# Chunk 0 of the Gram blocks at 64 columns, placed first in its group on the two borrowed PSUM banks

## The chip, the core and the metric

The kernel runs on one core of one Trainium2 chip. The metric is device time in microseconds (us), the median over several executions. Before the change it is 1001.87 us (three runs, 1001.54 to 1002.07).

## What is computed

One layer of a hybrid encoder block over 528 tokens (16 meta tokens and 512 real ones) of width 2048. One input projection feeds two branches: an RWKV-7 recurrence with 16 heads of 64, and a gated short convolution. Their outputs are concatenated and go through one output projection. The change touches only the recurrence, which per token and head is

```python
sa = einsum('bhvk,bhk->bhv', S, kk_t)
S  = S * w_t - sa[..., None] * b_t + v_t[..., None] * k_t
y_t = einsum('bhvk,bhk->bhv', S, r_t)
```

The first 16 tokens (the meta tokens) are dropped from the output, so for them only the state S matters, not y.

## The kernel before

**Chunks.** The recurrence is not run token by token. Tokens are laid out in `NCH` = 9 chunks of `CH` = 64: chunk 0 holds the 16 meta tokens and padding, chunks 1 to 8 the 512 real tokens. Heads are handled in 8 pairs; a pair fills the 128 partitions, one head on partitions 0 to 63 and the other on 64 to 127. `prepare(i)` makes for pair `i` two tiles: `ar` (decayed keys in half 0, receptance in half 1 of each chunk) and `bk` (two sets of decayed keys). For chunk 0 the receptance half is zeros: line 662 sets `ar[:, 0, 1]` to 0 with a memset on POOL.

**The Gram blocks.** For every chunk and head, `gram` multiplies 64 rows of `bk` (128 columns, the stationary weights) with 64 rows of `ar` (128 columns, streamed through) into a 128x128 block: 18 matmuls in float32 for each pair, which the trace records as 36 because each float32 matmul takes two passes. `masked` then multiplies the blocks with a causal mask on DVE and writes them to the SBUF tile `gt`. For chunk 0 the columns 64 to 127 of each block are zero before and after the mask, because the receptance half is zero, and nothing that is computed later reads those columns for its result.

**Where the blocks lie.** PSUM has eight banks. Pool `pm` has four of them (tag `main`) for the two accumulators of the running input projection and of the one before it; pool `pz` has two (`tz`); pool `pi` has one each of `misc` and `ser`. The nine chunks of one head take nine blocks of a quarter bank: four in a `tz` bank (`za`, chunks 0 to 3), four in `misc` or `ser` (`zc`, chunks 4 to 7) and the ninth in a bank borrowed from the projection (`ze`, chunk 8). With two heads that is six banks, two of them borrowed from `main`.

**What sets the order.** The order of TensorE's work is written by hand. The input projection (`main`, `steps`, line 328) is a generator that is stepped by `fill(ns)`, so that projection matmuls stand between the small steps of `prepare` and `invert`; a call fills a given number of modelled nanoseconds with them. A projection unit (names `ps_k`, `ps_r`, `ps_v`, `ps_g`, `ps_C` and so on) runs for about 11 us, then its one or two `main` banks are read by DVE (`scaled`, line 352), and the next unit needs free `main` banks. The queues of DVE, ACT and POOL are ordered by a planner at build time, from its own estimate of costs, priorities and of when each input is ready; `ahead()` and `tc.high_priority` raise priorities there. Each engine then runs its list in order.

**Lines that the change and the prediction speak of.** Line 677 is the `fill` ahead of the Gram group, line 703 the loop over chunks, lines 705 to 707 the masks, line 708 the `fill` behind them. Lines 714 to 718 are the next small products (`n2` into `misc` and `tz`, `zb` into `ser`), which need those banks back. Lines 746 and 751 send `gt` to DRAM by DMA: to the inversion of the 16x16 blocks, and to the store `opd`, from which the recurrence loads its operands. Lines 855 and 895, in `invert`, are the last reads of `gt` on TensorE; there are two `gt` buffers, one for even and one for odd pairs. Line 135 on POOL and DVE makes the low part of the projection's weights, out of what ACT casts in line 134. Line 460 sums squares at the start, with single-column float32 matmuls. Line 1005 is a product of the recurrence.

Of the kernel before, what the change touches and what calls it, by code (L numbers as in the profile page):

```python
# [9 lines left out]
F32 = mybir.dt.float32  # L10
# [8 lines left out]
P = 128  # L19
# [5 lines left out]
CH = 64  # L25
NCH = SEQ // CH + 1
# [51 lines left out]
def hymba_kernel(ctx: ExitStack, tc: tile.TileContext, xt, xtok, front, w_in, w_out, pv, lup, cst, msk, gf, out):  # L78
    nc = tc.nc
# [14 lines left out]
    def col(off, i=0):  # L94
        return pvt[:, off + i : off + i + 1]
# [69 lines left out]
    gmask = cs[:, C_GM : C_GM + 256].rearrange("p (h c) -> p h c", h=2)  # L165
    pm = ph1.enter_context(tc.tile_pool(name="pm", bufs=4, space=PSUM))
# [130 lines left out]
    with tc.issue_after(head):  # L297
        nc.vector.tensor_scalar(
            out=omm, in0=pvt[:, V_MU : V_MU + 33], scalar1=-1.0, scalar2=1.0, op0=ALU.mult, op1=ALU.add
        )  # L300
        for d, off in (
# [4 lines left out]
                out=d, in0=pvt[:, off : off + 8], scalar1=0.5, scalar2=None, op0=ALU.mult  # L306
            )
        nc.vector.tensor_scalar(
            out=hv[:, 4], in0=pvt[:, V_KA : V_KA + 8], scalar1=-0.5, scalar2=1.0, op0=ALU.mult, op1=ALU.add
# [241 lines left out]
    def fill(ns):  # L551
        while ns > 0:
            seen = len(ready)
            t = step()
            if t is None:
                return
            ns -= t
            if len(ready) > seen:
                ns += FW["evac"]
# [23 lines left out]
    def ahead():  # L583
        return tc.high_priority(offset=AHEAD)

    def c3(t):
        return t.rearrange("p (c s) -> p c s", s=CH)
# [39 lines left out]
    def prepare(i):  # L627
        p = i % 2
        until("k", i)
        k = got["k", i]  # L630
        ar = cq.tile([P, NCH, 2, CH], F32, tag="ar", name=f"ar{i}")
# [18 lines left out]
            out=bk[:, :, 1], in0=c3(k), scalar=hv[:, 2, i : i + 1], in1=c3(te), op0=ALU.mult, op1=ALU.mult  # L650
        )
        nc.gpsimd.tensor_scalar(
            out=ta, in0=ta, scalar1=hv[:, 3, i : i + 1], scalar2=hv[:, 4, i : i + 1], op0=ALU.mult, op1=ALU.add
        )
        nc.vector.scalar_tensor_tensor(
            out=ar[:, :, 0], in0=c3(k), scalar=col(V_KK, i), in1=e1[:, :, 0:CH], op0=ALU.mult, op1=ALU.mult
# [9 lines left out]
            out=ar[:, 1:NCH, 1], in0=c3(r), in1=e1[:, 1:NCH, 1 : CH + 1], op=ALU.mult  # L666
        )
        nc.vector.scalar_tensor_tensor(
            out=r, in0=r, scalar=hv[:, 5, i : i + 1], in1=ta[:, CH:LP], op0=ALU.mult, op1=ALU.mult
# [7 lines left out]
        fill(FW["gram_b" if p else "gram"] + shift)  # L677

        gt = cq.tile([P, 2, NCH, P], F32, tag=f"gt{p}", name=f"gt{i}")
        def gram(z, c, c0):  # L680
            for h, hs, ho in heads:
                nc.tensor.matmul(  # L682
                    z[h][:, c - c0],
                    bk[hs, c, h : h + 2, :].rearrange("p a s -> p (a s)"),
                    ar[hs, c].rearrange("p a s -> p (a s)"),
                    start=True, stop=True,
                )

        def masked(z, c0, c1):
            with ahead():  # L690
                for h in range(2):
                    nc.vector.tensor_tensor(  # L692
                        out=gt[:, h, c0:c1],
                        in0=z[h],
                        in1=gmask[:, h].unsqueeze(1).to_broadcast([P, c1 - c0, P]),
                        op=ALU.mult,
                    )


        za = [pz.tile([P, 4, P], F32, tag="tz", name=f"g{i}_0_{h}") for h in range(2)]  # L700
        zc = [pi.tile([P, 4, P], F32, tag=("misc", "ser")[h], name=f"g{i}_4_{h}") for h in range(2)]
        ze = [pm.tile([P, 1, P], F32, tag="main", name=f"g{i}_8_{h}") for h in range(2)]
        for c in range(NCH):
            gram((za, zc, ze)[c // 4], c, c // 4 * 4)
        masked(za, 0, 4)
        masked(zc, 4, 8)
        masked(ze, 8, 9)
        fill(FW["gram2"] - shift + 1300 * (i == 1) + 2000 * (i == 3))

        n2 = tr(f"n2{i}")  # L710
# [56 lines left out]
        def sub(x, r0, c0, dims):  # L767
            return bass.AP(tensor=x.tensor, offset=x.offset + r0 * 16 + c0, ap=[list(x.ap[0])] + dims)

        for m in (2, 4, 8):  # L770
            for b in range(16 // (2 * m)):
# [4 lines left out]
                    out=pq,  # L776
                    in0=sub(d, o, o + m, [[16, m], [0, m], [1, m]]),
                    in1=sub(y, o + m, o + m, [[0, m], [1, m], [16, m]]),
# [3 lines left out]
                    out=tq.rearrange("p (i j) -> p i j", i=m), in_=pq, op=ALU.add, axis=AX.X  # L782
                )
                nc.vector.tensor_tensor(
                    out=pq,
                    in0=sub(y, o, o, [[16, m], [0, m], [1, m]]),
                    in1=bass.AP(tensor=tq.tensor, offset=tq.offset, ap=[list(tq.ap[0]), [0, m], [1, m], [m, m]]),
# [274 lines left out]
    for i in range(0, NPAIR, 2):  # L1062
        invert([prepare(i), prepare(i + 1)])
# [155 lines left out]
    def here(t, n):  # L1219
        return xa[t][:, n * 512 : (n + 1) * 512] if n < 2 else xb[n - 2][:, t]  # L1220
# [151 lines left out]
    z = {}  # L1372
    for u, unit in enumerate(units):
        half, prod, g = unit
# [53 lines left out]
    with tc.manual_schedule(engines={mybir.EngineType.DVE, mybir.EngineType.Activation, mybir.EngineType.Pool}):  # L1428
# [16 lines left out]
        for part in range(2):  # L1445
# [7 lines left out]
            h = here(1, 2)[:, cols]  # L1453
# [73 lines left out]
```

## Time and profile before

| what | value |
|---|---|
| median of the runs | 1001.87 us |
| the profiled execution's own time | 999.8 us |
| its span, first to last instruction | 997.9 us |
| TensorE (PE) busy | 986.4 us, 99% of the span |
| DVE, ACT, POOL busy | 691.5, 412.7, 268.2 us |
| granted TensorE clock, mean | 0.997 of full speed |
| Gram matmuls (line 682) | 288 records in 8 groups, from 80.6 to 547.2 us |
| Gram masks on DVE (line 692) | 48: 32 of 128x512 and 16 of 128x128 |

A row of a timeline gives the start in us, the time in us until the last of the merged instructions ends, the engine (PE is the matmuls, PEld the weight loads), the line of the kernel, the operation with the tiles it writes and reads, shapes, and the count of merged records; a bracket is idle time before it and what ended it. Matmuls are pipelined: one record lasts longer than the distance to the next, so rates are read from the distance between starts.

### The profile page before, as it was taken

Reading aid. Unit: us, or ns where it says so; the run is one execution under the profiler, and the core shown is the slowest. Engines: PE = TensorE matmul, PEld = TensorE weight load, DVE = VectorE, ACT = ScalarE, POOL = GpSimd, SP = SyncE. Lnnn points to the kernel's source line nnn. Section 1 sums busy time; section 2 is a strip of 40 time slices with the busy share of each in tenths; the row PEclk is TensorE's granted clock in tenths of the full one; section 3 lists DMA queues with packets and bytes.
Section 4 is the critical chain, followed back from the end, with each engine's and each line's share of the span. In section 5 each row is a group of like instructions: output and inputs, shape, how many; then the busy total and the mean of one; then the engine's idle time right before and its main releaser. Section 6 shows DMA issues by size and latency. Waiting matters only on the chain.

```text
span 997.9 us, 22790 instructions
## 1 busy us (share of the span) xinstructions
PE 986.4 (99%) x9211; PEld 911.0 (91%) x9211; DVE 691.5 (69%) x1314; ACT 412.7 (41%) x770; POOL 268.2 (27%) x286
## 2 busy tenths in 40 slices
PE   9999999999999999999999999999999999999996
PEld 8999999999998999998999998989889898888885
DVE  7687975487765679735579735246555598999895
ACT  7554432353422534232534323233333325645553
POOL 0123323234322324222324222223242422011001
PEclk9999999999999999999999999999999999999998
DMA  9527485437683465854264854988783698698644
GB/s 337 155 70 198 112 218 150 115 105 179 149 226 108 107 178 128 221 148 118 84 180 119 224 142 125 355 259 281 219 262 94 195 260 229 212 297 218 143 102 168
DMA packets 184986, 179.48 MB, mean 180 GB/s; under 512 B 112177, under 2 KB 141617, under 8 KB 184369
## 3 DMA queue, kind: packets, MB, share of 16 engines
q1 hardware_dynamic: 182288, 169.12, 57.9%
q0 software_dynamic: 2304, 8.39, 4.9%
q8 instruction: 72, 1.18, 0.5%
q10 hardware_dynamic: 288, 0.52, 0.1%
q14 instruction: 34, 0.27, 0.1%
HBM read 139.28 MB, written 38.71 MB: 178 GB/s over the span
## 4 chain that ended last, share of the span: by engine, by line
PE 96%; DVE 1%; DMA 1%; issue 1%; POOL 0%; ACT 0%; DVEq 0%; POOLq 0%
PE ps_r L328 9%; PE ps_h L328 9%; PE ps_g L328 9%; PE ps_gc L328 9%; PE ps_B L328 9%; PE ps_v L328 9%; PE ps_C L328 8%; PE ps_k L328 8%; PE M L1243 8%; PE P L1243 4%; PE Q L1243 2%; PE g L682 2%; DMA ct<-opd 1%; PE ps_lora L328 1%; PE rz L958 1%; PE zs L1005 1%
## 5 line engine op out<-in xcount | busy, mean ns | idle before, releaser
L134 ACT CAST w<-wr 128x512 fp32r<-128x512 f32 x252 | 153.4, 619 | 281.0 <-PE ps_h L328 44.7
L135 POOL TENSOR_TENSOR w<-wr,w 128x512 fp32r<-128x512 f32 x119 | 165.8, 1395 | 371.5 <-ACT w L134 331.6
L135 DVE TENSOR_TENSOR w<-wr,w 128x512 fp32r<-128x512 f32 x133 | 99.2, 751 | 99.8 <-ACT w L134 99.6
L328 PE MATMUL ps_r<-xh,w 128*128 128x256 f32 (+1 forms) x512 | 95.2, 282 | 1.0 <-DVE gt L692 1.0
L328 PE MATMUL ps_k<-xh,w 128*128 128x256 f32 (+1 forms) x512 | 95.4, 284 | 0.0
L328 PE MATMUL ps_v<-xh,w 128*128 128x272 f32 (+1 forms) x512 | 95.4, 284 | 0.0
L328 PE MATMUL ps_h<-xh,w 128*128 128x258 f32 (+1 forms) x512 | 93.4, 282 | 0.0
L328 PE MATMUL ps_C<-xh,w 128*128 128x258 f32 (+1 forms) x512 | 93.2, 281 | 0.0
L328 PE MATMUL ps_g<-xh,w 128*128 128x258 f32 (+1 forms) x512 | 91.7, 280 | 0.0
L328 PE MATMUL ps_B<-xh,w 128*128 128x512 f32 x256 | 83.1, 394 | 0.0
L328 PEld LDWEIGHTS ps_r<-xh,w 128*128 128x128 f32 x512 | 80.2, 189 | 1.6 <-DVE gt L692 1.2
L328 PE MATMUL ps_gc<-xh,w 128*128 128x512 f32 x256 | 81.7, 393 | 0.0
L328 PEld LDWEIGHTS ps_k<-xh,w 128*128 128x128 f32 x512 | 80.3, 189 | 0.3
L328 PEld LDWEIGHTS ps_v<-xh,w 128*128 128x128 f32 x512 | 80.1, 189 | 0.3
L328 PEld LDWEIGHTS ps_C<-xh,w 128*128 128x128 f32 x512 | 79.6, 189 | 0.6
L328 PEld LDWEIGHTS ps_h<-xh,w 128*128 128x128 f32 x512 | 79.2, 189 | 0.7
L328 PEld LDWEIGHTS ps_g<-xh,w 128*128 128x128 f32 x512 | 79.2, 189 | 0.2
L328 PE MATMUL ps_k<-xl,w 128*128 128x256 f32 (+1 forms) x256 | 73.0, 285 | 0.0
L328 PE MATMUL ps_v<-xl,w 128*128 128x256 f32 (+1 forms) x256 | 72.5, 283 | 0.0
L328 PE MATMUL ps_g<-xl,w 128*128 128x256 f32 (+1 forms) x256 | 72.4, 283 | 0.0
L328 PE MATMUL ps_r<-xl,w 128*128 128x256 f32 (+1 forms) x256 | 72.1, 282 | 0.0
L328 PE MATMUL ps_C<-xl,w 128*128 128x256 f32 (+1 forms) x256 | 71.9, 281 | 0.0
(312 smaller groups left out, 2205.8 us busy)
## 6 DMA issues: line engine op xcount, KB each, us to landing
wr<-in_w_in_dram SPq DMA_DIRECT2D x126, 512.0 KB
ct<-opd SPq DMA_DIRECT2D x56, 320.0 KB
wo<-in_w_out_dram SPq DMA_DIRECT2D x21, 512.0 KB
opd<-gt SPq DMA_DIRECT2D x16, 576.0 KB
x<-in_w_out_dram POOLq DMA_DIRECT2D x16, 512.0 KB, 5.7
opd<-ar SPq DMA_DIRECT2D x8, 576.0 KB
opd<-bt SPq DMA_DIRECT2D x64, 64.0 KB
ct<-opd SPq DMA_DIRECT2D x16, 256.0 KB
```

The lines of the kernel that those rows point to most:

```text
L134: nc.scalar.copy(hi, rq)
L135: low[q] = eng.tensor_tensor(out=lo, in0=rq, in1=hi.bitcast(F32), op=ALU.subtract).ins
L328: nc.tensor.matmul(ps[r], ww[:, w], xx[:, kt, a:b], start=(kt == 0 and n == 0), stop=(kt == KT - 1 and n == 2))
L682: nc.tensor.matmul(z[h][:, c - c0], bk[hs, c, h : h + 2, :].rearrange("p a s -> p (a s)"), ar[hs, c].rearrange("p a s -> p (a s)"), start= ...
L958: nc.tensor.matmul(z[e][ho if e else hs, 0, k], ct[e][hs, k, o : o + CH], uv(e, k, hs, h) if part else st[hs, 4 * e + k], start=(part == 0 ...
L1005: nc.tensor.matmul(zs[hs, j], bb[:, h], uv(e, k, everything, h), start=True, stop=True)
L1243: nc.tensor.matmul(bank[s], left(prod, jj, m, s), w, start=(jj == 0 and n == 0), stop=(jj == 7 and n == 2))
```

## The change

Chunk 0 gets its own place. Its Gram matmuls stream only the 64 key columns of `ar`; the other 64 columns of its blocks in `gt`, which are zero, are set by a new memset on POOL, one for each pair. Chunk 0 goes to the two borrowed banks, now 64 columns wide, and is issued first; chunks 1 to 4 go to `tz`, chunks 5 to 8 to `misc` and `ser`. The masks follow in the same new order: chunk 0 first, on 64 columns, then the two groups of four.

```diff
         gt = cq.tile([P, 2, NCH, P], F32, tag=f"gt{p}", name=f"gt{i}")
+        nc.gpsimd.memset(gt[:, :, 0, CH:P], 0.0)
+
         def gram(z, c, c0):
             for h, hs, ho in heads:
                 nc.tensor.matmul(
                     z[h][:, c - c0],
                     bk[hs, c, h : h + 2, :].rearrange("p a s -> p (a s)"),
-                    ar[hs, c].rearrange("p a s -> p (a s)"),
+                    ar[hs, c].rearrange("p a s -> p (a s)") if c else ar[hs, c, 0],
                     start=True, stop=True,
                 )
 
-        def masked(z, c0, c1):
+        def masked(z, c0, c1, n=P):
             with ahead():
                 for h in range(2):
                     nc.vector.tensor_tensor(
-                        out=gt[:, h, c0:c1],
+                        out=gt[:, h, c0:c1, 0:n],
                         in0=z[h],
-                        in1=gmask[:, h].unsqueeze(1).to_broadcast([P, c1 - c0, P]),
+                        in1=gmask[:, h, 0:n].unsqueeze(1).to_broadcast([P, c1 - c0, n]),
                         op=ALU.mult,
                     )
...
-        ze = [pm.tile([P, 1, P], F32, tag="main", name=f"g{i}_8_{h}") for h in range(2)]
-        for c in range(NCH):
-            gram((za, zc, ze)[c // 4], c, c // 4 * 4)
-        masked(za, 0, 4)
-        masked(zc, 4, 8)
-        masked(ze, 8, 9)
+        ze = [pm.tile([P, 1, CH], F32, tag="main", name=f"g{i}_8_{h}") for h in range(2)]
+        gram(ze, 0, 0)
+        for c in range(1, NCH):
+            gram((za, zc)[c // 5], c, 1 + c // 5 * 4)
+        masked(ze, 0, 1, CH)
+        masked(za, 1, 5)
+        masked(zc, 5, 9)
```

## The prediction

> **What bounds the kernel now.** I read the page first, then the list of what TensorE waited for, then TensorE's busy time by stretch, then the timelines of PE, DVE and POOL around each of the eight Gram groups.
>
> ```profile
> span 997.9 us, 22790 instructions
> PE 986.4 (99%) x9211; PEld 911.0 (91%) x9211; DVE 691.5 (69%) x1314; ACT 412.7 (41%) x770; POOL 268.2 (27%) x286
> ...
> PE ps_r L328 <- DVE gt L692: 1.0, 1, 1.0
> PE rz L958 <- DMA ct<-opd: 0.5, 2, 0.3
> ...
> 60.00:600.00 540.00, 538.91 (x5160) 519.89 (x5159) 367.95 (x789) 208.40 (x381) 171.35 (x181) 1.00 0.58 150
> ```
>
> TensorE is the bound: in the stretch of 60 to 600 us, which holds every Gram group, it is busy for 538.91 of 540 us. So a change counts only by what it does to TensorE: fewer or shorter matmuls, a wait less, a wait more. Only one wait there is named, 1.0 us, and it is one on the Gram masks. The profiled execution took 999.8 us (span 997.9, and 1.9 around it), 2.07 less than the median of 1001.87; I sum differences on its timeline and carry them to the median.
>
> **The shorter matmuls.** The change halves the streamed columns of 16 float32 matmuls, two in each of 8 groups, but not their weights: these stay 128 columns. What sets the pace of a pass?
>
> ```profile
> 213.53 2.28 PE L682 MATMUL g<-ar,bk 64*128 64x128 f32 x36
> ...
> 45.54 0.70 PE L460 MATMUL pss<-cs,accd 128*128 128x1 f32 x5
> ...
> 638.22 1.18 PE L1005 MATMUL zs<-ct 128*64 128x64 f32 x32
> ```
>
> A Gram group is 36 records in 18 concurrent pairs (both heads at once), the last lasting 0.27 us, so 2.28 - 0.27 = 2.01 us from first start to last. That is 17 steps, the first a double one while the pipeline fills: 2.01 / 18 = 0.112 us a step, 0.223 for a chunk of two passes. Line 460 loads 128 weight columns for each pass too, but streams a single column: (0.70 - 0.25) / 4 = 0.112. The same pace with 1 column as with 128: the weight load sets it. Line 1005, with 64 weight columns and 64 streamed, goes at (1.18 - 0.22) / 16 = 0.060 (32 records in 16 pairs, the first step double again). So the bounds for a chunk 0 of 128 weight columns and 64 streamed are 0.112 a pass (no gain) and 0.060 (2 x 0.052 = 0.10 us a group, 0.83 in all). I take 0: line 460 has the same weight width, line 1005 has not. What line 460 doesn't show is 64 rows in place of 128. The Trainium skill, "TensorE: Matmul & The Clock Gate", section "LDWEIGHTS (loading the stationary operand)", fills that: a load costs by its columns, not its rows, columns/1.2 ns, an estimate of 107 ns a pass for 128; by it the sum has 0 here, and by line 1005's pace it would have -0.83.
>
> **The wait that goes.** Pair 2, in time order on PE and DVE:
>
> ```profile
> 217.80 0.29 PE L328 MATMUL ps_k<-xh,w 128*128 128x272 f32 x1
> 219.04 0.38 PE L328 MATMUL ps_r<-xh,w 128*128 128x256 f32 x1 [0.96 <-DVE gt L692]
> 219.26 0.28 PE L328 MATMUL ps_r<-xl,w 128*128 128x256 f32 x1
> ...
> 216.92 2.87 DVE L692 TENSOR_TENSOR gt<-g,cs 128x512 f32<-128x512 f32 x6
> 218.12 0.87 DVE L692 TENSOR_TENSOR gt<-g,cs 128x512 f32<-128x512 f32 x2
> ...
> L692 DVE TENSOR_TENSOR gt<-g,cs x48: 275/678/685, 82.9 to 550.4; 128x512 f32<-128x512 f32 x32, 128x128 f32<-128x128 f32 x16
> ```
>
> The unit `ps_r` begins in the borrowed banks. DVE comes to the six masks only at 216.92; the first narrow one is its fourth and ends at 218.12 + 0.87 = 218.99, and PE goes on 0.05 later. From the start at 217.80 the next should follow after 0.12 (the distance of such matmuls here: 272 columns); it follows after 1.24, and the one behind it after 0.22 in place of 0.12, while the pipeline fills again. Loss: 1.12 + 0.10 = 1.22 us.
>
> In the new order the narrow mask is first: it would end near 216.92 + 0.28 = 217.20, release near 217.25, needed at 217.92. The wait goes whole: **-1.22**. Next late there is nothing on PE that I can see. Bounds: 0, if DVE's list doesn't put the mask first, and -1.22. All that follows is moved ahead with PE, save what waits on a transfer: the line 958 waits above, 0.5 us, could grow at most by what was won.
>
> **The wait that comes.** Chunk 0 now needs the borrowed banks at the start of the group; before, chunk 8 needed them 16 pairs later, 16 x 0.112 = 1.8 us. They hold the unit before, until DVE has read it. Pairs 0, 1 and 7 are the tight ones:
>
> ```profile
> 80.61 2.28 PE L682 MATMUL g<-ar,bk 64*128 64x128 f32 x36
> 79.82 0.89 DVE L352 TENSOR_TENSOR pr_k<-ps_k,rs 128x256 f32<-128x256 f32 x4
> ...
> 122.33 2.28 PE L682 MATMUL g<-ar,bk 64*128 64x128 f32 x36
> 121.71 0.45 DVE L352 TENSOR_TENSOR pr_g<-ps_g,rs 128x256 f32<-128x256 f32 x2
> ...
> 545.16 0.71 PE L682 MATMUL g<-ar,bk 64*128 64x128 f32 x8
> 544.15 0.56 DVE L352 TENSOR_TENSOR pr_v<-ps_v,rs 128x256 f32<-128x256 f32 x3
> ...
> 396.11 0.38 PE L682 MATMUL g<-ar,bk 64*128 64x128 f32 x2
> 394.79 0.56 DVE L352 TENSOR_TENSOR pr_v<-ps_v,rs 128x256 f32<-128x256 f32 x3
> ```
>
> The reads end at 80.71, 122.16 and 544.71; with 0.05 for the release the banks are free at 80.76, 122.21 and 544.76, against 80.61, 122.33 and 545.16. So pair 0 waits 0.15 us, the others not. Queued behind the waiting matmul is the whole of TensorE. Pair 5 is the next tightest (395.35 against 396.11). **+0.15**; bounds 0 and, if the planner puts one more 0.7 us operation ahead of each of the three last reads, 0.85 + 0.58 + 0.30 = 1.73.
>
> **The masks.** DVE's long and narrow masks last 0.678 and 0.275 us: 0.403 for 384 columns, 1.05 ns a column. A run of six has its last start at 219.79 - 0.28 = 219.51, so four long and one narrow step make 2.59 us: 0.60 and 0.20 a step. A 64-wide one saves 0.067, an estimate: 0.13 a step; 16 of them save 1.07 us of DVE, which is busy for 69% and not the bound: 0. But two narrow ones now run ahead of the wide ones, so the other banks come free later: `misc` by 2 x 0.13 = 0.26, `ser` by 0.26 - 0.20 = 0.06 (one narrow mask stood ahead of it already). That counts where line 714 or 717 waits, in pair 1:
>
> ```profile
> 129.24 0.29 PE L714 MATMUL n_misc<-sq_h,ones 128*2 128x288 f32 x1
> 129.63 0.29 PE L715 MATMUL n_tz<-sq_l,ones 128*2 128x288 f32 x1
> 130.05 0.47 PE L717 MATMUL zb<-rk_h,ones 128*128 128x512 f32 x1
> ...
> 127.24 2.87 DVE L692 TENSOR_TENSOR gt<-g,cs 128x512 f32<-128x512 f32 x6
> ```
>
> PE goes from 129.63 to 130.05, 0.42 where 0.13 is usual here, since `ser` is read until about 129.9. The new order moves that by 0.06: **+0.06**; bounds -0.3 (the masks of chunk 0 run earlier, in one of DVE's gaps) and +0.26. Pair 3 is the next closest:
>
> ```profile
> 266.45 0.29 PE L714 MATMUL n_misc<-sq_h,ones 128*2 128x288 f32 x1
> ...
> 263.82 2.88 DVE L692 TENSOR_TENSOR gt<-g,cs 128x512 f32<-128x512 f32 x6
> ```
>
> There `misc` is read until 263.82 + 2 x 0.60 + 0.68 = 265.70, and 0.26 more fits ahead of 266.45.
>
> **The memset.** POOL gets 8 memsets of 128 columns; the nearest rows:
>
> ```profile
> L662 POOL MEMSET ar<- x8: 152/152/157, 29.0 to 507.4; 128x64 f32 x8
> ...
> 186.20 0.14 POOL L567 MEMSET tz<- 128x48 f32 x1
> 187.01 0.14 POOL L567 MEMSET ta<- 128x48 f32 x1 [0.67 <-PE t L895]
> ```
>
> 0.15 each for 64 columns, up to 0.3 for 128: at most 2.4 us of a POOL that is idle for 73%. The memset waits for the last read of the `gt` buffer two pairs before, which for pair 2 is line 895 near 187; the line 567 memsets wait for the same event, and the Gram group starts at 213.53, 26 us later. I take 0. If that cover is gone it is the third rival. No DMA is added or moved; the `gt` transfers wait on one engine more.
>
> **Sum.** 0 - 1.22 + 0.15 + 0.06 + 0 = -1.01 us: the profiled execution would be at 998.8, the median at 1001.87 - 1.01 = **1000.9**. Its own range is 1000.4 to 1001.3. A measurement here can tell about 0.2%, 2.0 us, from no change, so this is within it.
>
> **Rivals.**
> *The streamed columns set the pace* (line 1005's): 0.83 more is won, 1000.0. Against it is line 460, for it only that the heads here use half the rows each. The same page of the Trainium skill, section "Back-to-back issue gap", gives an isolated matmul N/2.4 + 2.5 ns: 56 at 128 columns and 29 at 64; at that ratio a chunk's 0.223 becomes an estimated 0.116, 0.86 us less over the groups, against which line 460's pace speaks here.
> *The change doesn't free the banks earlier*: the planner keeps the chunk 0 masks where the narrow ones were, since it, not the source, orders DVE. Then +0.15 + 0.06 stay: 1002.1.
> *The borrowed banks come too late* in all three tight pairs: 1.73 for 0.15, 1002.4. DVE's lists ahead of those reads are full of 0.7 us operations, but nothing in the change asks for another one there.
> *Slower: the memset stands behind a waiting operation on POOL.*
>
> ```profile
> POOL w L135 <- ACT w L134: 331.6, 82, 8.0
> ...
> 82.99 0.15 POOL L662 MEMSET ar<- 128x64 f32 x1 [1.94 <-PE g L682]
> 86.37 1.29 POOL L135 TENSOR_TENSOR w<-wr,w 128x512 fp32r<-128x512 f32 x1 [3.23 <-ACT w L134]
> ...
> 86.67 0.29 PE L714 MATMUL n_misc<-sq_h,ones 128*2 128x288 f32 x1
> ```
>
> POOL stands for 331.6 us behind ACT's casts, and runs in order. Put behind the operation at 86.37 in pair 0, the memset would end at 87.8; if masks wait for it, `misc` comes free 0.26 + 2 x 0.60 + 0.68 = 2.14 later, at 89.95, and line 714 starts at 90.0 and not at 86.67: +3.3, so 1004.2. It decides from the memset ending after 84.5, and eats the gain from 85.5. Against it: `gt` is free long before, and POOL has 1.94 us of idle time just ahead.
>
> **How the numbers follow.** Forecast 0.48, streamed columns 0.12, banks not freed 0.10, banks too late 0.12, memset 0.18. Faster by over 0.2% (below 999.9) is about half of the second case and a tail of the first, where the planner's new lists help elsewhere too: 0.12. Slower by over 0.2% (above 1003.9) is the memset case and a little of the bank case: 0.21. The rest, 0.67, is within. The range, 999.4 to 1004.0, takes in the streamed-columns case and reaches to the edge of the memset case.
>
> **What would show it.** Right: the Gram groups still last 2.28 us, `ps_r` of pair 2 follows `ps_k` without a wait, a wait of about 0.15 us ahead of pair 0's first Gram matmul, memsets well ahead of their masks. Wrong: groups of about 2.17 us (streamed columns), masks of chunk 0 behind the others, waits of more than 0.3 us on line 352 ahead of a Gram group, a mask released by POOL. A new wait of over 2 us anywhere else on TensorE, from the planner's new lists, would break the sum without breaking its terms.

## The result, and the profile after

| | before | after |
|---|---|---|
| median, same chip | 1001.25 us (17 runs, 999.99 to 1002.22) | 1003.43 us (17 runs, 1002.00 to 1005.03) |
| ratio, 95% interval | 1 | 1.0021 (1.0014 to 1.0027) |
| profiled execution's own time | 999.8 us | 1002.2 us |

The change costs 2.2 us. The forecast was a gain of 1.0.

The page of the changed kernel, its span and engines:

```profile
span 1000.3 us, 22800 instructions
PE 987.5 (99%) x9211; PEld 911.1 (91%) x9211; DVE 692.8 (69%) x1314; ACT 411.5 (41%) x770; POOL 268.0 (27%) x294
```

Its list of what TensorE waited for (total us, times, longest):

```profile
PE g L684 <- DVE pr_g L352: 1.5, 2, 1.2
...
PE ps_C L328 <- issue: 0.5, 1, 0.5
PE z L874 <- issue: 0.3, 1, 0.3
```

The 1.0 us wait of `ps_r` on a Gram mask is gone. In its place Gram matmuls (now line 684) wait for DVE's reads of the projection banks, on the line 352 that the prediction watched. The timeline of PE in the changed kernel, pair 1's Gram group, then pair 2's group and its `ps_r`:

```profile
123.25 0.43 PE L684 MATMUL g<-ar,bk 64*128 64x64 f32 x2 [0.24 <-DVE pr_g L352]
124.93 0.94 PE L684 MATMUL g<-ar,bk 64*128 64x64 f32 x12 [1.25 <-DVE pr_g L352]
...
217.24 2.28 PE L684 MATMUL g<-ar,bk 64*128 64x64 f32 x36
...
221.50 0.29 PE L328 MATMUL ps_k<-xh,w 128*128 128x272 f32 x1
221.63 0.28 PE L328 MATMUL ps_r<-xh,w 128*128 128x256 f32 x1
221.75 0.28 PE L328 MATMUL ps_r<-xl,w 128*128 128x256 f32 x1
```

Three readings. In pair 1 the first head's chunk 0 starts at 123.25, the second head's bank comes free only for 124.93. Pair 2's group lasts 2.28 us as before, though its chunk 0 streams 64 columns. And `ps_r` follows `ps_k` after 0.13 us, where it took 1.24 before.

**Where the time went.** Both kernels have 9211 matmul records, so the k-th of one can be set against the k-th of the other. The table gives the growth of that shift, in us, between fixed matmuls of the first profile of before; the last column is the shift of the very last matmul. The rows below the first are the experiments of the next section.

| kernel | start, to 10 us | pair 0, to 121 | pair 1's group, to 128 | pair 1's lines 714 to 718, to 132 | to 173 | inversion of pairs 0 and 1, to 213 | pair 2, to 221 | rest | all |
|---|---|---|---|---|---|---|---|---|---|
| after | +0.45 | +0.17 | +1.95 | +0.12 | +0.39 | +0.63 | -1.20 | -0.14 | +2.37 |
| e1, chunk 0 first | +0.88 | +0.20 | +1.68 | +0.25 | +0.35 | +0.55 | -1.20 | -0.11 | +2.60 |
| e2, 64 columns | +1.20 | -0.04 | -0.05 | +0.38 | 0.00 | +0.41 | -0.08 | -0.51 | +1.31 |
| e3, memset | +0.40 | -0.02 | 0.00 | +0.35 | 0.00 | +0.44 | +0.01 | +0.03 | +1.21 |
| e4, reads first | +0.03 | +0.31 | +0.75 | +0.43 | +0.37 | +0.60 | -1.20 | +0.26 | +1.55 |
| e5, not in pair 0 | -0.14 | -0.01 | 0.00 | +0.23 | 0.00 | +0.87 | -1.20 | +1.26 | +1.02 |
| e6, pair 0 alone | +0.54 | +0.19 | 0.00 | +1.73 | +0.36 | +1.13 | +0.02 | +0.32 | +4.30 |
| e7, pair 2 alone | +0.36 | 0.00 | 0.00 | +0.01 | 0.00 | +1.00 | -1.20 | +0.29 | +0.46 |
| e8, before again | +0.96 | -0.03 | 0.00 | -0.03 | 0.00 | +1.06 | -0.03 | -0.14 | +1.79 |
| e9, `te` ahead | +0.67 | +0.20 | 0.00 | -0.36 | 0.00 | 0.00 | -1.20 | -0.82 | -1.51 |

The row of e8 is the unchanged kernel, profiled once more: its start and its inversion stage alone move by 0.96 and 1.06 us. So these two columns tell nothing of an edit (the first profile of before was a short execution, 999.8 us against a median of 1001.25). The "rest" moved by only 0.14 in e8; what moves it by up to 1.26 in other rows was not followed, and nothing is read from it. The column of lines 714 to 718 moves by some 0.4 us with the memset alone (e3), so only what is well above that counts there. The others agree to 0.1 us wherever kernels have the same order at that place, but for 0.14 in pair 0 (e4) and for 0.27 in pair 1's group (1.95 in the changed kernel, 1.68 in e1). They say of the change: pair 0 +0.17, pair 1 +1.95 + 0.12, up to 173 +0.39, pair 2 -1.20, together +1.43; the medians differ by 2.18, and the other 0.75 isn't placed.

**Why pair 1.** The timeline of DVE in the changed kernel, up to pair 1's masks (start, duration):

```profile
106.28 0.22 DVE L784 TENSOR_REDUCE tt<-prod 72x16 f32<-72x64 f32 x1
...
107.01 1.35 DVE L787 TENSOR_TENSOR prod<-y,tt 72x64 f32<-72x64 f32 x1
...
112.93 0.74 DVE L648 SCALAR_TENSOR_TENSOR te<-ta,e 128x576 f32<-128x576 f32 x1
...
120.88 0.69 DVE L602 TENSOR_TENSOR rk_l<-r,rk_h 128x512 fp32r<-128x512 f32 x1 [0.74 <-ACT rk_h L601]
122.17 0.69 DVE L135 TENSOR_TENSOR w<-wr,w 128x512 fp32r<-128x512 f32 x1 [0.60 <-ACT w L134]
122.78 0.42 DVE L352 TENSOR_TENSOR pr_g<-ps_g,rs 128x256 f32<-128x256 f32 x1
123.11 1.30 DVE L733 STREAM_TRANSPOSE bt<-bk 128x512 f32<-128x512 f32 x2
124.33 0.45 DVE L352 TENSOR_TENSOR pr_g<-ps_g,rs 128x256 f32<-128x256 f32 x2
...
129.86 2.73 DVE L694 TENSOR_TENSOR gt<-g,cs 128x64 f32<-128x64 f32 x6
```

The same stretch of DVE before:

```profile
105.19 0.22 DVE L781 TENSOR_REDUCE tt<-prod 72x16 f32<-72x64 f32 x1
105.44 0.27 DVE L784 TENSOR_TENSOR prod<-y,tt 72x64 f32<-72x64 f32 x1
...
108.38 0.75 DVE L648 SCALAR_TENSOR_TENSOR te<-ta,e 128x576 f32<-128x576 f32 x1
...
118.47 0.68 DVE L602 TENSOR_TENSOR rk_l<-r,rk_h 128x512 fp32r<-128x512 f32 x1
119.55 0.69 DVE L135 TENSOR_TENSOR w<-wr,w 128x512 fp32r<-128x512 f32 x1 [0.40 <-ACT w L134]
120.16 0.71 DVE L730 STREAM_TRANSPOSE bt<-bk 128x512 f32<-128x512 f32 x1
120.79 0.39 DVE L352 TENSOR_TENSOR pr_g<-ps_g,rs 128x256 f32<-128x256 f32 x1
121.10 0.69 DVE L730 STREAM_TRANSPOSE bt<-bk 128x512 f32<-128x512 f32 x1
```

DVE runs the same operations in another order. `te` (line 648, the first step of pair 1's decayed keys) stood ahead of most reads of `ps_v`; now it stands behind them all. Everything that `te` feeds is late, and with it the reads of `ps_g`: the last ended at 121.71 + 0.45 = 122.16 before and ends at 124.78 now, and the masks begin at 129.86 against 127.24. Besides, both transposes now stand between the reads of the two banks; before, one stood ahead of the first read and one between. Chunk 0, now first, needs both heads' banks at the group's start, and TensorE stands. Nothing in the diff touches line 648.

### The profile page after: what moved, and what is told of

Read it like the earlier page. It is cut to its first block, busy times and chain, and to the rows that moved or that the text cites. A ratio compares the mean times of both kernels' runs of the same rounds, so it can differ in the third digit from the quotient of the medians.

```text
span 1000.3 us, 22800 instructions
## 1 busy us (share of the span) xinstructions
PE 987.5 (99%) x9211; PEld 911.1 (91%) x9211; DVE 692.8 (69%) x1314; ACT 411.5 (41%) x770; POOL 268.0 (27%) x294
## 3 DMA queue, kind: packets, MB, share of 16 engines
q8 instruction: 72, 1.18, 0.5%
## 4 chain that ended last, share of the span: by engine, by line
PE 92%; DMA 2%; DVE 2%; issue 2%; POOL 1%; ACT 0%; SPq 0%; DVEq 0%; POOLq 0%
PE ps_h L328 9%; PE ps_r L328 9%; PE ps_B L328 9%; PE ps_k L328 9%; PE ps_v L328 9%; PE ps_gc L328 8%; PE ps_C L328 8%; PE M L1246 8%; PE ps_g L328 7%; PE P L1246 4%; PE Q L1246 2%; PE g L684 2%; PE ps_lora L328 1%; PE rz L961 1%; PE zs L1008 1%
```

## The experiments

The theory after the result: the new place of chunk 0 in pair 1 needs the banks early, and a redrawn list on DVE brings them late. Rivals: the 64 columns, the memset, variation from execution to execution.

### The parts, one at a time (e1, e2, e3)

e1: chunk 0 first, at 128 columns, without the memset.

```diff
-        for c in range(NCH):
-            gram((za, zc, ze)[c // 4], c, c // 4 * 4)
-        masked(za, 0, 4)
-        masked(zc, 4, 8)
-        masked(ze, 8, 9)
+        gram(ze, 0, 0)
+        for c in range(1, NCH):
+            gram((za, zc)[c // 5], c, 1 + c // 5 * 4)
+        masked(ze, 0, 1)
+        masked(za, 1, 5)
+        masked(zc, 5, 9)
```

> Position alone: chunk 0 first in the group on the borrowed banks, at 128 columns, no memset. Theory A (the borrowed banks are needed at the start of the group, and in pair 1 DVE has not read them): the wait ahead of pair 1's Gram group is 1.5 to 2.1 us as in the changed kernel, the 1.1 us wait of pair 2 is gone, and the total is 1 to 2.5 us above before. Rival B (the 64-column matmuls make the planner draw other lists): no wait in pair 1, total at or up to 1.2 us below before. Rival C (the memset holds up POOL): as B.

e2: 64 columns and the memset, with chunk 0 on the borrowed banks, but issued and masked last.

```diff
+        nc.gpsimd.memset(gt[:, :, 0, CH:P], 0.0)
...
-                    ar[hs, c].rearrange("p a s -> p (a s)"),
+                    ar[hs, c].rearrange("p a s -> p (a s)") if c else ar[hs, c, 0],
...
+        for c in range(1, NCH):
+            gram((za, zc)[c // 5], c, 1 + c // 5 * 4)
+        gram(ze, 0, 0)
+        masked(za, 1, 5)
+        masked(zc, 5, 9)
+        masked(ze, 0, 1, CH)
```

> 64 columns and memset alone: chunk 0 is issued and masked last, on the borrowed banks. Theory A: no wait ahead of pair 1's group, the 1.1 us wait of pair 2 stays, total within 0.7 us of before. Rival B: pair 1 waits 1.5 us or more and the total is about 2 us above before. Rival C: as B, with a mask or a weight split that waits for POOL. If streamed columns set the pace, each group is 0.1 us shorter than 2.28.

e3: the memset alone, in the kernel before.

```diff
+        nc.gpsimd.memset(gt[:, :, 0, CH:P], 0.0)
```

> The memset alone, in the kernel before (its 128 columns are written again by the masks). Theory A and rival B: within 0.3 us of before, no new wait on TensorE. Rival C: 1 us or more above before, with masks that end later in pairs 0, 2 and 4.

| kernel | median | before, same chip | ratio (95%) |
|---|---|---|---|
| e1 | 1002.68 | 1001.19 | 1.0016 (1.0006 to 1.0025) |
| e2 | 1001.11 | 1001.19 | 1.0000 (0.9990 to 1.0009) |
| e3 | 1001.66 | 1001.19 | 1.0003 (0.9994 to 1.0013) |

TensorE's waits, first e1 (the Gram wait is there), then e2, then e3 (in both the old wait is still there, and no new one is over 0.6 us):

```profile
PE g L682 <- DVE pr_g L352: 1.2, 1, 1.2
```

```profile
PE ps_r L328 <- DVE gt L694: 0.9, 1, 0.9
```

```profile
PE ps_r L328 <- DVE gt L694: 1.0, 1, 1.0
```

The loss comes with the place of chunk 0 alone; what the columns and the memset are worth, these medians can't tell from nothing. e3's median is 0.47 us above before, more than the 0.3 that was expected, but its interval takes in no change at all.

The trace of e2 shows more than its median does. Pair 2's Gram group there:

```profile
215.43 2.23 PE L684 MATMUL g<-ar,bk 64*128 64x128 f32 x36
```

It is 0.05 us shorter than 2.28, half of the 0.1 that was expected if the streamed columns set the pace, and so are all eight groups of e2: with chunk 0 last, one of its two passes takes 0.059 us from start to start, where the others take 0.112. That makes 0.4 us in all. In the changed kernel, with chunk 0 first, a step at the start of the group is shorter by the same 0.05, but the second step behind it takes 0.165 in place of 0.112, and the group keeps its 2.28.

The memsets and the masks in the changed kernel, grouped (count, shortest, median and longest in ns, first and last start):

```profile
L680 POOL MEMSET gt<- x8: 204/205/209, 26.6 to 457.8; 128x128 f32 x8
...
L694 DVE TENSOR_TENSOR gt<-g,cs x48: 185/676/691, 82.7 to 552.3; 128x512 f32<-128x512 f32 x32, 128x64 f32<-128x64 f32 x16
```

The first memset starts 56 us ahead of the first mask, the last 94 ahead of the last.

### The reads ahead of the transposes (e4)

The changed kernel with pair 1's transposes issued behind the reads of `ps_g`, one swap in DVE's list.

```diff
...
-            nc.vector.transpose(bt[:, :, :, :, a], bk[:, 0 : NCH - 1, 2 * a].rearrange("p c (t s) -> p c t s", t=2))
+            with tc.issue_after(reads["g0"]) if i == 1 else nullcontext():
+                nc.vector.transpose(bt[:, :, :, :, a], bk[:, 0 : NCH - 1, 2 * a].rearrange("p c (t s) -> p c t s", t=2))
```

> The changed kernel, with one thing moved: in pair 1 DVE reads the second borrowed bank ahead of its two transposes, not behind them. Theory A: the second read ends about 1.2 us earlier, the wait in pair 1 falls from 1.6 to 0.4 us or less, and the total is about 1.2 us below the changed kernel's. If the wait in pair 1 only stands for time that is lost anyway further on, the total stays.

1001.99 against 1001.19, ratio 1.0009 (0.9999 to 1.0018): 0.80 us above before, where the changed kernel is 2.18 above. That is about what theory A gave, though the two intervals overlap. TensorE's waits:

```profile
PE n_misc L718 <- DVE gt L695: 0.4, 1, 0.4
...
PE g L685 <- DVE pr_g L352: 0.2, 1, 0.2
```

The Gram group's loss falls from 1.95 to 0.75, but the product behind it (line 718 here) now waits 0.4 us for the masks, which are late too. The two transposes are only part of it; DVE as a whole is late.

### Where the list is redrawn (e5, e6, e7)

The new order of chunk 0, at 128 columns and without the memset, in some pairs only: e5 in pairs 1 to 7, e6 in pair 0, e7 in pair 2. The other pairs keep the old order.

```diff
+        if i > 0:
+            gram(ze, 0, 0)
+            for c in range(1, NCH):
+                gram((za, zc)[c // 5], c, 1 + c // 5 * 4)
+            masked(ze, 0, 1)
+            masked(za, 1, 5)
+            masked(zc, 5, 9)
+        else:
+            for c in range(NCH):
+                gram((za, zc, ze)[c // 4], c, c // 4 * 4)
...
```

(e6 has `if i == 0:`, e7 `if i == 2:`.)

> Chunk 0 first, at 128 columns, in pairs 1 to 7; pair 0 stays as before. The lists that the planner draws for ACT, POOL and SP are those of before, DVE's too but for the masks' own places. Theory A1 (position hurts in pair 1 only together with the lists that pair 0's new order brings about): no wait ahead of pair 1's group (at most 0.2 us), pair 2's 1.1 us wait gone, total about 1 us below before. Rival A2 (position alone hurts in pair 1): the wait of 1.2 us or more is there, total 0.5 to 2 us above before.

> Chunk 0 first, at 128 columns, in pair 0 alone. DVE's list is redrawn ahead of pair 1 as in the changed kernel, but pair 1 needs the borrowed banks only for its last chunk. A1: DVE reads pair 1's second bank near 124.7 as in the changed kernel, PE waits there for 0 to 0.7 us, pair 2's wait of 1.1 us stays; total 0.3 to 1.2 us above before. If the redrawn list alone costs the time: 1.5 us or more in pair 1, total about 2.5 us above before.

> Chunk 0 first, at 128 columns, in pair 2 alone: all lists as before but for pair 2's masks. All theories that name pair 2's wait as the only gain: 1.2 us off at pair 2 in the trace, no other change on TensorE, total 0.8 to 1.3 us below before (0.999). If other pairs' order helps too, the e5 kernel is faster than this one.

| kernel | median | before, same chip | ratio (95%) |
|---|---|---|---|
| e5, all but pair 0 | 1000.12 | 1001.27 | 0.9988 (0.9979 to 0.9997) |
| e6, pair 0 alone | 1003.79 | 1001.27 | 1.0028 (1.0016 to 1.0039) |
| e7, pair 2 alone | 1000.33 | 1001.27 | 0.9990 (0.9981 to 0.9999) |

e5 and e7 came as theory A1 and the theory of pair 2's wait had them: 1.15 and 0.94 us below before, with -1.20 at pair 2 in the traces. The two are too close to tell whether the order of other pairs helps. In e5 a wait of 0.7 us is new on line 1251, far behind the Gram groups; whether the edit brings it was not followed.

DVE in e5, pair 1: `te` in its old place, the reads ended by 122.02.

```profile
108.22 0.74 DVE L648 SCALAR_TENSOR_TENSOR te<-ta,e 128x576 f32<-128x576 f32 x1
...
121.57 0.45 DVE L352 TENSOR_TENSOR pr_g<-ps_g,rs 128x256 f32<-128x256 f32 x2
```

PE in e5, where chunk 0 comes first in pair 1 and the group does not wait:

```profile
122.18 2.28 PE L682 MATMUL g<-ar,bk 64*128 64x128 f32 x36
```

DVE in e6, where nothing but pair 0's order is changed: pair 1's `te` is late, as in the changed kernel.

```profile
112.76 0.74 DVE L648 SCALAR_TENSOR_TENSOR te<-ta,e 128x576 f32<-128x576 f32 x1
...
129.69 1.87 DVE L692 TENSOR_TENSOR gt<-g,cs 128x512 f32<-128x512 f32 x3
```

And TensorE's waits in e6:

```profile
PE n_misc L722 <- DVE gt L692: 1.5, 1, 1.5
...
PE ps_r L328 <- DVE gt L692: 0.9, 1, 0.9
```

This is the turn of the study. For e6 the smaller loss that was expected (0.3 to 1.2 us) missed, and the other one named, a redrawn list that costs by itself (about 2.5), came: 1003.79 - 1001.27 = 2.52. The edit that costs the time stands in pair 0; the place that pays is pair 1. With the old order in pair 1 (e6) the late masks stop line 714's product for 1.5 us; with the new order (e1, and the changed kernel) the late reads stop the Gram group instead. The lateness is the same, and chunk 0's place only decides where it shows. My first theory was half wrong: on a list that is not redrawn, the new order in pair 1 needs no banks that are not there (e5). In the traces, DVE's order between the two Gram groups is the same redraw in the changed kernel, in e1 and in e6, while in e2, e5 and e7 that stretch is as before, apart from the masks' own places. The column up to 173 of the table goes with it: +0.35 to +0.39 in the four kernels with `te` late, nothing in the others. It is one late projection matmul; what that waits for was not followed. Nor was why the planner sets `te` late when pair 0's order changes.

### The same kernel once more (e8)

> The kernel before, once more, for a second profile: how far its waits outside the Gram groups (the first 12 us, the inversion of pairs 0 and 1 at 170 to 182 us) vary by themselves. If they vary by 0.3 us or more, differences of that size there are no effect of the change.

Its profiled execution took 1001.58 us, its span 999.7 us. Its row stands in the table; one of its waits, against none there in the first profile:

```profile
PE z L871 <- issue: 0.7, 1, 0.7
```

### `te` put back (e9)

The changed kernel whole, with the priority of one operation raised in pair 1.

```diff
-        nc.vector.scalar_tensor_tensor(out=te, in0=ta, scalar=1.0, in1=e2, op0=ALU.add, op1=ALU.mult)
+        with ahead() if i == 1 else nullcontext():
+            nc.vector.scalar_tensor_tensor(out=te, in0=ta, scalar=1.0, in1=e2, op0=ALU.add, op1=ALU.mult)
```

> The changed kernel, with the one operation te (line 648) of pair 1 raised in priority, so that it stands ahead of the reads of ps_v in DVE's list again, as in the kernel before. Theory A, the late place of te in the redrawn list makes all of DVE late in pair 1: te starts at 108 to 110 us (112.93 in the changed kernel, 108.38 before), the last read of ps_g ends by 122.5 (124.8), pair 1's Gram group waits 0.3 us at most (1.5) and line 720 0.3 at most, pair 2 keeps its gain of 1.1 to 1.2; the time is 1.5 to 2.3 us below the changed kernel's, about 1000.0 to 1001.0 against a before of 1001.3. Theory B, the lateness comes from other places of the redrawn list: te is early, but the last read of ps_g still ends after 124 and pair 1 still loses over 1 us; 1002 to 1003.5. Theory C, raising te redraws the list once more and moves the wait elsewhere: pair 1 is free of it, and a wait of over 0.5 us that the changed kernel does not have stands on another line.

999.02 against 1001.09, ratio 0.9980 (0.9971 to 0.9989): the best of all kernels here, below both. DVE's timeline:

```profile
106.52 0.22 DVE L785 TENSOR_REDUCE tt<-prod 72x16 f32<-72x64 f32 x1
...
107.25 0.27 DVE L788 TENSOR_TENSOR prod<-y,tt 72x64 f32<-72x64 f32 x1
...
109.00 0.75 DVE L649 SCALAR_TENSOR_TENSOR te<-ta,e 128x576 f32<-128x576 f32 x1
...
118.66 0.69 DVE L602 TENSOR_TENSOR rk_l<-r,rk_h 128x512 fp32r<-128x512 f32 x1
119.94 0.69 DVE L135 TENSOR_TENSOR w<-wr,w 128x512 fp32r<-128x512 f32 x1 [0.59 <-ACT w L134]
...
122.11 0.45 DVE L352 TENSOR_TENSOR pr_g<-ps_g,rs 128x256 f32<-128x256 f32 x2
...
127.64 2.73 DVE L695 TENSOR_TENSOR gt<-g,cs 128x64 f32<-128x64 f32 x6
```

PE's timeline, pair 1:

```profile
123.19 2.28 PE L685 MATMUL g<-ar,bk 64*128 64x64 f32 x36
```

`te` starts at 109.00, the last read of `ps_g` ends at 122.56, the group runs its 2.28 us without a wait, and the product `zb` (line 720 in the changed kernel) waits for nothing. Theory A held, but for 0.06 us at that read, at a better total than it gave (1000.0 to 1001.0); theories B and C did not. Its lead over e5 is inside the two intervals.

The edit names one operation, but the planner moved others with it: `ta`, `sq_l`, one `w` and one transpose on DVE, and a `w` each on ACT and POOL, most of them back to where they stood before. What stayed is as telling: up to `te` the two kernels' lists on DVE are the same, with five operations moved against before, the first of them a `w` in pair 0's group; in e9 the loss is gone all the same. So these five moves alone don't make it.

How `te`'s place makes 2.5 us: between the two reductions `tt` (106.28 in the changed kernel, 106.52 in e9) and the operation `w` at 122.17 and 119.94, DVE runs the same operations in 15.89 and 13.42 us. Two of the losses can be read. `rk_l` waits 0.74 for ACT, with nothing left in the list to fill the gap. And `prod` lasts 1.35 us for 0.27. POOL in the changed kernel:

```profile
106.90 1.34 POOL L135 TENSOR_TENSOR w<-wr,w 128x512 fp32r<-128x512 f32 x1 [0.85 <-ACT w L134]
113.79 1.45 POOL L652 TENSOR_SCALAR ta<-ta,hv 128x576 f32<-128x576 f32 x1 [5.55 <-DVE te L648]
```

POOL in e9:

```profile
109.86 0.83 POOL L653 TENSOR_SCALAR ta<-ta,hv 128x576 f32<-128x576 f32 x1 [3.57 <-DVE te L649]
110.66 2.24 POOL L135 TENSOR_TENSOR w<-wr,w 128x512 fp32r<-128x512 f32 x1
```

With `te` late, POOL's list has its `w` ahead of `ta`, and the small DVE product that starts 0.11 us into it ends with it: 107.01 + 1.35 = 108.36, POOL's end 106.90 + 1.34 = 108.24. That is 1.08 us, with 0.74 for `rk_l` 1.82 of 15.89 - 13.42 = 2.47. The rest was not split, and it is a balance: the write of `bk` in line 659 takes 1.84 us for 0.75 in e9, the product of line 668 0.74 for 1.77. That the two stand in each other's way is read from rows of the traces (more of them at the end), not from a run of its own.

## Why the prediction was wrong, point by point

**The shorter matmuls, 0: right for this order.** The groups that do not wait still last 2.28 us with 64 streamed columns (pair 2 of the changed kernel, pair 1 of e9), and the rival's 0.83 us did not come. The reason given, that the weight load sets the pace of every pass, is not quite what the traces show: with chunk 0 last (e2) each group is 0.05 us shorter, since one of its two passes goes at 0.059, near line 1005's 0.060. That the changed kernel gains nothing depends on chunk 0's place too, which the prediction did not see. The other passes keep 0.112; the Trainium skill, "TensorE: Matmul & The Clock Gate", "LDWEIGHTS (loading the stationary operand)", gives a load by its columns, an estimate of 0.107 us for 128, and the traces agree with that for these passes.

**The wait that goes, -1.22: right,** measured -1.20 in each of the six kernels with the new order in pair 2, and 0.94 on the medians in e7, which changes nothing else. That settles also the rival of the banks not freed.

**The wait that comes: the step that failed.** The term was +0.15 for pair 0 and 0 for pair 1, "122.21 [...] against 122.33". Pair 0 came as forecast, +0.17 (+0.19 and +0.20 in e1, e6 and e9, +0.31 in e4). Pair 1 was priced on DVE's list of before: "nothing in the change asks for another one there". Even its upper bound, one more 0.7 us operation ahead of the read (0.58 for pair 1), was far too low, since the whole list moved: the reads end 2.6 us later and TensorE loses 1.95 there, 0.12 behind it and 0.39 up to 173. The rival of the banks that come too late had the right mechanism on TensorE, and 1002.4, but for three pairs at 0.3 to 0.85 each; it was one pair, and pairs 5 and 7 lost nothing. What it lacked was the cause: an edit in pair 0 redraws another pair's list. The prediction's last sentence named "the planner's new lists", but as something that would show elsewhere, and gave it no price. The sign that was named for it came, a wait of more than 0.3 us on line 352 ahead of a Gram group. That the range held 1003.4 was luck: its slow side was drawn for another mechanism, the memset.

**The masks, +0.06:** +0.12 in the changed kernel and -0.36 in e9, in a column that moves by +0.35 in e3 with no mask changed: small, and no more can be said.

**The memset, 0: not contradicted.** e3 measured 1.0003 (0.9994 to 1.0013), and the mask's wait behind POOL, the rival that carried the slow side, did not come.

**The sum.** By the columns that repeat: -1.20 + 0.17 for what was foreseen, -1.0 as forecast; and +2.46 in pair 1 and behind it, which was not. e9 is the forecast with its silent premise restored: its edits are those of the change, its list in pair 1 is close to the old one, and it comes out 2.1 us below before, of which -1.20 + 0.20 = -1.0, the forecast's own terms, is seen in the columns that repeat; the other 1.1 isn't placed.

## What to carry to other kernels

Where a planner orders the queues, a change of order is two changes: the one in the diff, and a new list for every engine from there on. Compare the lists of the two kernels as built, the far pairs and stages too, before a term is priced on the timeline of before; if they can't be had, put the cost of one redrawn stage into the range. And when a wait appears, follow the releasing engine back through the operations that changed their place, and test the one that feeds the late ones; here it was not the first that had moved. One raised priority there gave back more than the change had lost.

## What was not expected of the hardware

A DVE product of 72x64 with two inputs took 1.35 us beside a POOL `tensor_tensor` and 0.27 us without it; in the changed kernel it starts while POOL's runs and ends 0.12 us behind it. That kernel has 16 such products (line 787): twelve take 0.26 or 0.27 us, four 1.18 to 1.35, and these four are the ones that start while a `w` runs on POOL, each ending 0.13 us or less behind it. This agrees with the Trainium skill, "SBUF — State Buffer", "Who interferes with whom": a DVE instruction with two SBUF inputs contends with a GpSimd instruction that reads SBUF, and the port pair that they share is an exclusive lock. But two of the twelve, at 377.82 and 526.87, lie within the span of a `tensor_scalar` on POOL (line 639) and still take 0.26 us, so not every such overlap costs; why is open. Here an off-path engine that is 27% busy cost DVE 1.08 us by its list alone.

The start (to 10 us) and the inversion of pairs 0 and 1 moved by 0.96 and 1.06 us between two profiles of the same kernel, with no edit; what picks between them stays open.
